# Attention probabilities and v as plain fp32: one product with the values of both heads per key block, in a two-layer trunk on one core

## The chip, the cores and the metric

One core of a Trainium2 chip runs the whole program. The metric is the device time of one execution in microseconds (us); the kernel before was run three times. The engines are named as in the profile: PE (TensorE, products and transposes), PEld (PE's weight loads), DVE (VectorE), ACT (ScalarE), POOL (GpSimd) and SP (SyncE, which issues the DMAs).

## The reference

A trunk of two residual layers over 1024 tokens of width 1024. Layer 0 mixes tokens by a chunked gated MLP, layer 1 by attention; both are followed by an MLP of width 4096. The change touches attention alone: 16 heads of 64, three dilation patterns g, each with its own q, k and v. A block of 128 queries sees its own block of keys and, where there is one, the block before it.

```python
B_PATTERNS = ((128, 1), (512, 4), (2048, 16))
...
    s = jnp.einsum('bnqrhe,bnkrhe->bnrhqk', qb, kb, preferred_element_type=jnp.float32) * (E ** -0.5)
    s = s + bias
    s = jnp.where(valid[None, :, None, None], s, NEG)
    m = jnp.max(s, axis=-1, keepdims=True)
    p = jnp.exp(s - m)
    l = jnp.sum(p, axis=-1, keepdims=True)
    o = jnp.einsum('bnrhqk,bnkrhe->bnqrhe', p / l, vb.astype(jnp.float32))
...
    wts = jax.nn.softmax(jnp.stack(lses, axis=0), axis=0)[..., None]
    o = jnp.sum(wts * jnp.stack(outs, axis=0), axis=0)
```

The products that the change touches are those of the probabilities p with vb, without the division by l, which the kernel does later when it merges the three patterns.

## The kernel before, in words

Everything is fp32 in memory. A tile of type fp32r holds a rounded fp32 number that PE takes as one operand. To keep the precision, a number x is split into hi, x as fp32r, and lo, what is left, as fp32r again: `split` (lines 102 and 103) writes hi by a cast on ACT and lo by a subtraction on DVE. The large products take three of the four combinations of hi and lo (line 1134 for the projections).

Attention works in 24 rounds, `order`: 8 pairs of heads (hp), and in each the patterns 2, 1, 0. Two streams of work are woven together by a list of slots, 8 for a round. The first is `project()`: it makes q, k and v of the later rounds, one step being the three products of 512 columns for one block k (psq, psk, psv). The second, `attend`, puts its functions into a slot at one of three positions. When a slot is run, the functions of positions 0 and 1 are called, then three steps of `project()`, then those of position 2, then three steps more. The framework may shift an instruction by a few places from that.

For a round, `values()` (at the round's start, position 2) transposes vT of both heads, 128 columns of both together, into two PSUM banks (psvt, kind "tr", of which there are two) and splits them into v. Before, v has 256 columns for a block of keys, in the order hi of head 0, lo of head 0, lo of head 1, hi of head 1, so that 128 neighbouring columns hold hi and lo of one head. Then for each of the two heads e:

- `scores(m)` (position 0) makes the scores of query blocks 2m and 2m+1 (sc, lines 1207 and 1208), DVE adds the bias and takes the extreme (line 1214), ACT takes Exp (p, line 1216).
- `transposes(m)` (position 2) transposes a pack of 3 or 4 blocks of p into a "tr" bank (pT, lines 1239 and 1242) and splits it into pThi and pTlo. A pack has 512 columns, or 384; patterns 0 and 1 have four packs for a head, pattern 2 has two.
- `weighted(m)` (position 1, one slot later) multiplies the pack with v into the head's two PSUM banks pv (line 1262). The stationary operand is hi and lo of v, 128 columns, the moving one 128 or 256 columns of pThi, then of pTlo. So 64 rows of pv hold the product with hi of v, the other 64 that with lo of v. After the last pack, ACT copies one half of the rows to oT (line 1279), and DVE adds the other half (line 1280), for each of the two banks.

After the three patterns `merge` scales the oT tiles and adds them up.

Of the kernel before, what the change touches and what calls it, by code (L numbers as in the profile page):

```python
# [35 lines left out]
def trunk(ctx: ExitStack, tc: tile.TileContext, x, c, ada_w, ada_b, ln_g, ln_b, a_w_in, a_b_in,  # L36
# [1010 lines left out]
    def attention(before):  # L1047
# [6 lines left out]
        with ExitStack() as ph:  # L1054
# [113 lines left out]
            def attend(n, oT_of):  # L1168
# [5 lines left out]

                @at(base, 2)
                def values():
                    my["v"] = vs = qp.tile([P, NT, 4, HEAD], F32R, name=f"v_{hp}_{g}", tag="v")
                    for b in range(2):
                        pst = bank("tr", f"psvt_{hp}_{g}_{b}")
                        for t in range(4):  # L1180
                            t0 = (4 * b + t) * P
                            T.transpose(pst[:, t * P : (t + 1) * P], my["vT"][:, t0 : t0 + P], ident[:])
                        split(vs[:, 4 * b : 4 * b + 4, 0:4:3, :], vs[:, 4 * b : 4 * b + 4, 1:3, :],
                              pst[:].rearrange("p (t e c) -> p t e c", e=2, c=HEAD))

                for e in range(2):
                    h = 2 * hp + e
                    rows = slice(e * HEAD, (e + 1) * HEAD)
                    probs, pvs, st = {}, [], dict(begun=[False, False])

                    def scores(m, e=e, h=h, rows=rows, probs=probs, st=st):
                        if m == 0:
                            if e == 0:
                                my["stat"] = qp.tile([P, 2, 2, NT], F32, name=f"stat_{hp}_{g}", tag="stat", bufs=3)
                            st["bias"] = qp.tile([P, width], F32, name=f"bias_{h}_{g}", tag="bias")
                            G.tensor_scalar(st["bias"][:], (far if g == 2 else near)[:],
                                            -8.0 * DILATION[g] * 2.0 ** (-8.0 * (h + 1) / N_HEADS), 1.0, ALU.mult, ALU.mult)
                        scb, used = bank("sc", f"sc_{h}_{g}_{m}"), 0
                        stat = my["stat"]
                        spans = []  # L1200
                        for t in (2 * m, 2 * m + 1):
                            w = 2 * P if has[t] else P
                            sl = slice(used, used + w)
                            used += w
                            k0 = (t - 1) * P if has[t] else t * P
                            tq, keys = slice(t * P, (t + 1) * P), my[f"k{e}"]
                            T.matmul(scb[:, sl], my[f"q{e}"][:, tq], keys[:, k0 : k0 + w], start=True, stop=False)
                            T.matmul(scb[:, sl], my["qlo"][e][:, tq], keys[:, k0 : k0 + w], start=False, stop=True)  # L1208
                            spans.append((t, w, sl))
                        for t, w, sl in spans:  # L1210
                            pr = qp.tile([P, 2 * P], F32, name=f"p_{h}_{g}_{t}", tag="p", bufs=4)
                            col = (t % 2) * 4 + t // 2 if g == 1 else t
                            nm, l = stat[:, 0, e, col : col + 1], stat[:, 1, e, col : col + 1]
                            V.tensor_tensor_reduce(out=pr[:, 0:w], in0=scb[:, sl], in1=st["bias"][:, width - w :], scale=-0.125, scalar=3e38,  # L1214
                                                   op0=ALU.add, op1=ALU.min, accum_out=nm)
                            A.activation(pr[:, 0:w], pr[:, 0:w], AF.Exp, bias=nm, scale=-1.0, accum_out=l)  # L1216
                            probs[t] = pr


                    if g == 0:  # L1220
                        packs = [[(2 * m, True, 0), (2 * m + 1, m < 3, 2 * P)] for m in range(4)]
                        when = [1, 2, 3, 3]
                    elif g == 1:
                        packs = [[(2 * m, True, 0), (2 * m + 1, False, 2 * P)] for m in range(4)]
                        when = [0, 1, 2, 3]
                    else:
                        packs = [[(4 * m + t, False, t * P) for t in range(4)] for m in range(2)]
                        when = [1, 3]
                    total = [0, 0]
                    for t, nxt, _ in sum(packs, []):  # L1230
                        for b in {t // 4, (t + nxt) // 4}:
                            total[b] += 2
                    st["left"] = total
                    pT = {}

                    def transposes(m, h=h, probs=probs, packs=packs, pT=pT):
                        pst = bank("tr", f"pT_{h}_{g}_{m}")
                        for t, nxt, o in packs[m]:
                            T.transpose(pst[:, o : o + P], probs[t][:, P : 2 * P] if has[t] else probs[t][:, 0:P], ident[:])
                            end = o + P  # L1240
                            if nxt:
                                T.transpose(pst[:, o + P : o + 2 * P], probs[t + 1][:, 0:P], ident[:])
                                end = o + 2 * P
                        hi = work.tile([P, HALF], F32R, name=f"pThi_{h}_{g}_{m}", tag="h")
                        lo = qp.tile([P, HALF], F32R, name=f"pTlo_{h}_{g}_{m}", tag="pTlo")
                        split(hi[:, 0:end], lo[:, 0:end], pst[:, 0:end])
                        pT[m] = (hi, lo)

                    def weighted(m, e=e, h=h, rows=rows, packs=packs, pT=pT, pvs=pvs, st=st):
                        if m == 0:  # L1250
                            pvs.extend(bank("pv", f"pv_{h}_{g}_{b}") for b in range(2))
                        begun, left = st["begun"], st["left"]
                        for t, nxt, o in packs[m]:
                            stt = my["v"][:, t, 2 * e : 2 * e + 2, :].rearrange("p a c -> p (a c)")
                            for x_ in pT[m]:
                                pieces = [(t * P, o, P * (1 + nxt))]
                                if nxt and t % 4 == 3:
                                    pieces = [(t * P, o, P), ((t + 1) * P, o + P, P)]
                                for q0, o_, w_ in pieces:
                                    b = q0 // HALF  # L1260
                                    left[b] -= 1
                                    T.matmul(pvs[b][:, q0 % HALF : q0 % HALF + w_], stt, x_[:, o_ : o_ + w_],  # L1262
                                             start=not begun[b], stop=left[b] == 0, skip_group_check=True)
                                    begun[b] = True
                        if m < len(packs) - 1:
                            return
                        oT = oT_of(e)
                        main, rest = (slice(0, 64), slice(64, P)) if e == 0 else (slice(64, P), slice(0, 64))
                        for b in range(2):
                            if g == 0:  # L1270
                                dst = oT[rows, b * HALF : (b + 1) * HALF]
                                sa, sb = pvs[b][rest, :], pvs[b][main, :]
                            elif g == 1:
                                dst = by_pos(oT[rows, :], g)[:, 2 * b : 2 * b + 2, :]
                                sa, sb = (pvs[b][r, :].rearrange("p (r i) -> p r i", r=2) for r in (rest, main))
                            else:
                                dst = by_pos(oT[rows, :], g)[:, 4 * b : 4 * b + 4, :, :]
                                sa, sb = (pvs[b][r, :].rearrange("p (a b i) -> p a b i", a=4, b=2) for r in (rest, main))
                            A.copy(dst, sa)
                            V.tensor_tensor(dst, dst, sb, op=ALU.add)  # L1280

                    for m in range(4):
                        at(base + 4 * e + m, 0)(lambda m=m, f=scores: f(m))
                    for m, w in enumerate(when):
                        at(base + 4 * e + w, 2)(lambda m=m, f=transposes: f(m))
                        at(base + 4 * e + w + 1, 1)(lambda m=m, f=weighted: f(m))
# [179 lines left out]
```

## Time and profile before

| what | value |
|---|---|
| time, median of 3 runs | 2845.51 us (2842.47 to 2847.93) |
| span of the profiled execution | 2841.6 us; its own device time is not given apart from the three runs |
| granted clock of PE, mean | 0.992 |
| PE busy | 2752.7 us, 97% of the span, 13290 products |
| DVE busy | 1944.5 us, 68% |
| ACT busy | 1413.9 us, 50% |
| POOL busy | 220.1 us, 8% |
| DMA | 384.15 MB, 135 GB/s on average |

The span goes from the first to the last instruction of the profiled execution. Engines work side by side, so busy times don't add up to the span. Products on PE overlap one another in their records: what one costs is seen in the distance between starts, not in its duration. In a list of groups a row has the line, engine, operation, out<-in names, shape and count, then the busy time and the mean duration in ns, then the idle time of the engine before them and what ended it. In a timeline a row has the start, the duration and the instruction. Names are those of the program without the buffer number.

### The profile page before, as it was taken

The numbers are of one execution on the slowest core, as the hardware profiler recorded it, in microseconds if no ns is written. First come the engines' busy times: TensorE is split into PE (matmuls) and PEld (weight loads), VectorE is DVE, ScalarE is ACT, GpSimd is POOL, SyncE is SP. The second block draws the span as 40 slices with busy tenths as digits, with TensorE's granted clock in tenths as the row PEclk, the third lists the DMA queues.
The fourth block names the chain that finished last, engine by engine and source line by source line (L and its number), as shares of the span: only waits on it lengthen the run. The fifth ranks groups of instructions, "written<-read, shape, count | busy, mean of one in ns | idle before, by whom it ended". The sixth has DMA issues, their size and how long they took to land.

```text
span 2841.6 us, 36856 instructions
## 1 busy us (share of the span) xinstructions
PE 2752.7 (97%) x13290; PEld 2277.9 (80%) x13290; DVE 1944.5 (68%) x3485; ACT 1413.9 (50%) x2613; POOL 220.1 (8%) x163
## 2 busy tenths in 40 slices
PE   6999999999999999999999999999999999999997
PEld 5777878887888878888888888888877788878886
DVE  6786798777877674656555555555659976577776
ACT  3334375555434455555555555555564755544431
POOL 1021000000000043101000000010201000000000
PEclk9999999999999999999999999999999999999999
DMA  7533346668846343212121212121315564485561
GB/s 253 171 109 106 119 152 223 216 219 277 286 153 201 126 148 105 61 39 68 38 61 39 69 31 69 38 69 31 91 39 178 170 208 158 151 303 189 171 214 60
DMA packets 300186, 384.15 MB, mean 135 GB/s; under 512 B 47532, under 2 KB 172884, under 8 KB 300004
## 3 DMA queue, kind: packets, MB, share of 16 engines
q1 hardware_dynamic: 300004, 381.80, 42.0%
q8 instruction: 104, 1.70, 0.2%
q14 instruction: 78, 0.64, 0.1%
HBM read 297.77 MB, written 83.97 MB: 134 GB/s over the span
## 4 chain that ended last, share of the span: by engine, by line
PE 73%; DVE 11%; DMA 7%; ACT 5%; issue 2%; POOL 2%; SPq 0%; DVEq 0%; ACTq 0%; POOLq 0%
PE psd L938 21%; PE psua L782 10%; PE psv L1134 8%; PE psq L1134 7%; PE psk L1134 5%; PE psuc L782 5%; DMA adaw<-in_ada_w_dram 3%; PE psd_wout L356 3%; PE psub L782 2%; PE pv L1262 2%; PE psd_wo L356 2%; ACT p L1216 1%; DVE adaacc L128 1%; PE psu L356 1%; PE sc L1208 1%
## 5 line engine op out<-in xcount | busy, mean ns | idle before, releaser
L782 PE MATMUL psua<-right,left 128*128 128x512 f32 x1536 | 364.0, 391 | 3.4 <-ACT right L102 1.8
L938 PE MATMUL psd<-rhi,lhi 128*128 128x512 f32 x896 | 351.0, 392 | 2.1 <-ACT part L813 2.1
L938 PE MATMUL psd<-rlo,lhi 128*128 128x512 f32 x896 | 350.9, 392 | 1.2 <-DVE rlo L103 1.1
L938 PE MATMUL psd<-rhi,llo 128*128 128x512 f32 x896 | 350.5, 391 | 0.0
L782 PEld LDWEIGHTS psua<-right,left 128*128 128x128 f32 x1536 | 287.3, 188 | 65.5 <-DVE right L103 3.1
L1216 ACT ACTIVATE p<-p,stat 128x128 f32<-128x128 f32 (+1 forms) x384 | 170.4, 445 | 237.6 <-DVE stat L1214 235.7
L1134 PE MATMUL psv<-hT,wv_hi 128*128 128x512 f32 x768 | 246.0, 401 | 3.2 <-DVE qlo L103 3.2
L1134 PE MATMUL psq<-hT,wq_hi 128*128 128x512 f32 x768 | 246.3, 402 | 0.0
L1134 PE MATMUL psk<-hT,wk_hi 128*128 128x512 f32 x768 | 246.0, 401 | 0.0
L103 DVE TENSOR_TENSOR pTlo<-pT,pThi 128x512 fp32r<-128x512 f32 (+1 forms) x160 | 98.2, 621 | 179.1 <-ACT pThi L102 178.5
L938 PEld LDWEIGHTS psd<-rhi,lhi 128*128 128x128 f32 x896 | 169.3, 189 | 38.4 <-ACT part L813 2.9
L938 PEld LDWEIGHTS psd<-rlo,lhi 128*128 128x128 f32 x896 | 169.1, 189 | 37.0 <-DVE rlo L103 2.2
L938 PEld LDWEIGHTS psd<-rhi,llo 128*128 128x128 f32 x896 | 169.2, 189 | 35.3
L782 PE MATMUL psuc<-right,left 128*128 128x512 f32 x768 | 188.9, 392 | 0.0
L128 DVE SCALAR_TENSOR_TENSOR adaacc<-adaw,silu_c,adaacc 128x512 f32<-128x512 f32 x168 | 133.4, 805 | 64.1 <-DMA adaw<-in_ada_w_dram 63.4
L782 PEld LDWEIGHTS psuc<-right,left 128*128 128x128 f32 x768 | 144.4, 189 | 30.4 <-DVE right L103 0.5
L1214 DVE CUSTOM_DVE_ANT_0 p<-sc,bias 128x128 f32<-128x128 f32 (+1 forms) x384 | 119.7, 347 | 68.6 <-PE sc L1208 66.2
L1134 PEld LDWEIGHTS psv<-hT,wv_hi 128*128 128x128 f32 x768 | 135.6, 189 | 26.1 <-issue 2.8
L1134 PEld LDWEIGHTS psk<-hT,wk_hi 128*128 128x128 f32 x768 | 136.5, 189 | 22.6
L1134 PEld LDWEIGHTS psq<-hT,wq_hi 128*128 128x128 f32 x768 | 135.7, 189 | 22.2
L1134 PE MATMUL psq<-hT,wq_lo 128*128 128x512 f32 x384 | 151.4, 394 | 0.0
L1134 PE MATMUL psv<-hT,wv_lo 128*128 128x512 f32 x384 | 150.6, 392 | 0.0
(250 smaller groups left out, 5843.1 us busy)
## 6 DMA issues: line engine op xcount, KB each, us to landing
lraw<-forms SPq DMA_DIRECT2D x112, 512.0 KB, 3.7
adaw<-in_ada_w_dram SPq DMA_DIRECT2D x192, 256.0 KB, 3.2
up<-in_mlp_w_up_dram SPq DMA_DIRECT2D x64, 512.0 KB, 3.8
forms<-s SPq DMA_DIRECT2D x128, 256.0 KB, 2.4
rraw<-in_mlp_w_down_dram SPq DMA_DIRECT2D x64, 512.0 KB, 4.5
forms<-part SPq DMA_DIRECT2D x96, 256.0 KB, 2.5
spill<-acc SPq DMA_DIRECT2D x24, 512.0 KB, 2.7
wq_raw<-in_b_w_qkv_dram SPq DMA_DIRECT2D x24, 512.0 KB, 3.7
```

Of the source, the lines that this page charges most:

```text
L103: return first, lo_engine.tensor_tensor(lo, src, hi, op=ALU.subtract)
L128: ins = V.scalar_tensor_tensor(acc[:], raw[:], silu_c[:, k : k + 1], acc[:], ALU.mult, ALU.add)
L356: T.matmul(dst, s[a], m[b], start=(n == 0), stop=(n == last))
L782: T.matmul(acc, w[:, a, k, :], right[p][:, b, k, :], start=p in (1, 2, 5) and k + a + b == 0, stop=k == 3 and a == 1, skip_group_check=True)
L938: T.matmul(sums[kind, m][:], l[a][:, k, m * P : (m + 1) * P], r[b][:, k, :], start=p in (1, 5, 2, 3) and kp + k + a + b == 0, stop=kp == K ...
L1134: T.matmul(p[:], wu[a][:, k * P : (k + 1) * P], hT[half][b][:, k, :], start=k + c_ == 0, stop=k == KD - 1 and c_ == 2)
L1208: T.matmul(scb[:, sl], my["qlo"][e][:, tq], keys[:, k0 : k0 + w], start=False, stop=True)
L1214: V.tensor_tensor_reduce(out=pr[:, 0:w], in0=scb[:, sl], in1=st["bias"][:, width - w :], scale=-0.125, scalar=3e38, op0=ALU.add, op1=ALU.m ...
L1216: A.activation(pr[:, 0:w], pr[:, 0:w], AF.Exp, bias=nm, scale=-1.0, accum_out=l)
L1262: T.matmul(pvs[b][:, q0 % HALF : q0 % HALF + w_], stt, x_[:, o_ : o_ + w_], start=not begun[b], stop=left[b] == 0, skip_group_check=True)
```

## The change

- v is one fp32 tile with 128 columns for a block of keys, the 64 of head 0 and the 64 of head 1; one copy on ACT for a bank takes the place of cast and subtraction.
- The transposed probabilities are one fp32 tile, pTs. One copy takes the place of cast and subtraction, on ACT for an odd pack and on DVE for an even one.
- A pack has one product with v for each piece where it had two. The stationary operand is v of both heads, the moving one the probabilities of the head e; only the 64 rows of pv that belong to e are used.
- Those rows are copied from PSUM to oT in one step, by ACT for bank 0 and by DVE for bank 1.

```diff
                 def values():
-                    my["v"] = vs = qp.tile([P, NT, 4, HEAD], F32R, name=f"v_{hp}_{g}", tag="v")
+                    my["v"] = vs = qp.tile([P, NT, P], F32, name=f"v_{hp}_{g}", tag="v")
...
-                        split(vs[:, 4 * b : 4 * b + 4, 0:4:3, :], vs[:, 4 * b : 4 * b + 4, 1:3, :],
-                              pst[:].rearrange("p (t e c) -> p t e c", e=2, c=HEAD))
+                        A.copy(vs[:, 4 * b : 4 * b + 4, :].rearrange("p t c -> p (t c)"), pst[:])
...
-                            total[b] += 2
+                            total[b] += 1
...
-                        hi = work.tile([P, HALF], F32R, name=f"pThi_{h}_{g}_{m}", tag="h")
-                        lo = qp.tile([P, HALF], F32R, name=f"pTlo_{h}_{g}_{m}", tag="pTlo")
-                        split(hi[:, 0:end], lo[:, 0:end], pst[:, 0:end])
-                        pT[m] = (hi, lo)
+                        pT[m] = work.tile([P, HALF], F32, name=f"pTs_{h}_{g}_{m}", tag="h")
+                        (A.copy if m % 2 else V.tensor_copy)(pT[m][:, 0:end], pst[:, 0:end])
...
-                            stt = my["v"][:, t, 2 * e : 2 * e + 2, :].rearrange("p a c -> p (a c)")
-                            for x_ in pT[m]:
...
+                            stt = my["v"][:, t, :]
...
+                                T.matmul(pvs[b][:, q0 % HALF : q0 % HALF + w_], stt, pT[m][:, o_ : o_ + w_],
+                                         start=not begun[b], stop=left[b] == 0, skip_group_check=True)
...
-                            A.copy(dst, sa)
-                            V.tensor_tensor(dst, dst, sb, op=ALU.add)
+                            (V.tensor_copy if b else A.copy)(dst, src)
```

The rows below stand in the order of one engine's program, with the line, the instruction and the size of what it writes; numbers at the end of a name tell tiles apart. The first place is on PE, where the first pack of head 0 in pattern 1 is weighted. Before:

```order
L1207 MATMUL sc_1_1_9245<-k_0_1_8858,q_0_1_8628 128x256
L1208 MATMUL sc_1_1_9245<-k_0_1_8858,qlo_1_8453 128x256
L1262 MATMUL pv_1_0_9256<-pThi_1_0_9232,v_1_9213 128x256
L1262 MATMUL pv_1_0_9256<-pTlo_1_0_9233,v_1_9213 128x256
L1262 MATMUL pv_1_0_9256<-pThi_1_0_9232,v_1_9213 128x128
L1262 MATMUL pv_1_0_9256<-pTlo_1_0_9233,v_1_9213 128x128
L1134 MATMUL psq_0_0_9203<-hT_0_0_8565,wq_0_hi 128x512
```

Four products of the pack stand between the scores and the projection. On PE now:

```order
L1206 MATMUL sc_1_1_9211<-k_0_1_8856,q_0_1_8628 128x256
L1207 MATMUL sc_1_1_9211<-k_0_1_8856,qlo_1_8453 128x256
L1258 MATMUL pv_1_0_9222<-pTs_1_0_9200,v_1_9183 128x256
L1258 MATMUL pv_1_0_9222<-pTs_1_0_9200,v_1_9183 128x128
L1134 MATMUL psq_0_0_9173<-hT_0_0_8565,wq_0_hi 128x512
```

Two products of the program are left, at the same place. The second place is on DVE, around v and the first pack of the same round (ISA on L1214, later L1213, is the score reduction). Before:

```order
L103 TENSOR_TENSOR qlo_0_8454<-psq_0_1_9121,q_0_0_9120 64x512
L1280 TENSOR_TENSOR oT_2_8998<-oT_2_8998,pv_2_1_9086 64x4x2x64
L103 TENSOR_TENSOR v_1_9213<-psvt_1_0_9214,v_1_9213 128x4x128
L103 TENSOR_TENSOR v_1_9213<-psvt_1_1_9221,v_1_9213 128x4x128
L103 TENSOR_TENSOR pTlo_1_0_9233<-pT_1_0_9228,pThi_1_0_9232 128x384
L1214 ISA p_1_2_9250,stat_1_9172<-sc_1_1_9245,bias_1_9173 128x128
```

The two subtractions for v and the one for the pack stand ahead of the next score reduction. On DVE now:

```order
L1274 COPY oT_2_8984<-pv_2_1_9068 64x4x2x64
L103 TENSOR_TENSOR qlo_0_8454<-psq_0_1_9099,q_0_0_9098 64x512
L1244 COPY pTs_1_0_9200<-pT_1_0_9196 128x384
L1213 ISA p_1_2_9216,stat_1_9148<-sc_1_1_9211,bias_1_9149 128x128
L1213 ISA stat_1_9148 128x1
```

The subtractions for v are gone, the copy of the pack stands where its subtraction stood, and the copy to oT takes the place of the addition. On ACT at the same place, before:

```order
L1216 ACTIVATE p_1_1_9183,stat_1_9172<-p_1_1_9183,stat_1_9172 128x256
L1279 COPY oT_2_8998<-pv_2_1_9086 64x4x2x64
L102 CAST v_1_9213<-psvt_1_0_9214 128x4x2x64
L102 CAST v_1_9213<-psvt_1_1_9221 128x4x2x64
L102 CAST pThi_1_0_9232<-pT_1_0_9228 128x384
L1216 ACTIVATE p_1_2_9250,stat_1_9172<-p_1_2_9250,stat_1_9172 128x128
```

Between the two Exp (ACTIVATE) stand four copies or casts. On ACT now:

```order
L1215 ACTIVATE p_1_1_9159,stat_1_9148<-p_1_1_9159,stat_1_9148 128x256
L1183 COPY v_1_9183<-psvt_1_0_9184 128x512
L1183 COPY v_1_9183<-psvt_1_1_9190 128x512
L1215 ACTIVATE p_1_2_9216,stat_1_9148<-p_1_2_9216,stat_1_9148 128x128
L1215 ACTIVATE p_1_3_9219,stat_1_9148<-p_1_3_9219,stat_1_9148 128x256
```

Only the two copies of v are left between them; the copy of bank 1 to oT and that of the even pack are on DVE.

More of the change, by code (lines that the diff above doesn't have):

```diff
@@ L1253, in weighted @@
                         for t, nxt, o in packs[m]:
-                            stt = my["v"][:, t, 2 * e : 2 * e + 2, :].rearrange("p a c -> p (a c)")
-                            for x_ in pT[m]:
[L1256 to L1264, printed above, removed]
+                            stt = my["v"][:, t, :]
+                            pieces = [(t * P, o, P * (1 + nxt))]
+                            if nxt and t % 4 == 3:
+                                pieces = [(t * P, o, P), ((t + 1) * P, o + P, P)]
+                            for q0, o_, w_ in pieces:
+                                b = q0 // HALF
+                                left[b] -= 1
+                                T.matmul(pvs[b][:, q0 % HALF : q0 % HALF + w_], stt, pT[m][:, o_ : o_ + w_],
+                                         start=not begun[b], stop=left[b] == 0, skip_group_check=True)
+                                begun[b] = True
                         if m < len(packs) - 1:
@@ L1267, in weighted @@
                         oT = oT_of(e)
-                        main, rest = (slice(0, 64), slice(64, P)) if e == 0 else (slice(64, P), slice(0, 64))
                         for b in range(2):
@@ L1271, in weighted @@
                                 dst = oT[rows, b * HALF : (b + 1) * HALF]
-                                sa, sb = pvs[b][rest, :], pvs[b][main, :]
+                                src = pvs[b][rows, :]
                             elif g == 1:
                                 dst = by_pos(oT[rows, :], g)[:, 2 * b : 2 * b + 2, :]
-                                sa, sb = (pvs[b][r, :].rearrange("p (r i) -> p r i", r=2) for r in (rest, main))
+                                src = pvs[b][rows, :].rearrange("p (r i) -> p r i", r=2)
                             else:
                                 dst = by_pos(oT[rows, :], g)[:, 4 * b : 4 * b + 4, :, :]
-                                sa, sb = (pvs[b][r, :].rearrange("p (a b i) -> p a b i", a=4, b=2) for r in (rest, main))
-                            A.copy(dst, sa)
-                            V.tensor_tensor(dst, dst, sb, op=ALU.add)
+                                src = pvs[b][rows, :].rearrange("p (a b i) -> p a b i", a=4, b=2)
+                            (V.tensor_copy if b else A.copy)(dst, src)
                     for m in range(4):
```

## The prediction

> **What bounds the kernel now.** I read the page's totals first, then the busy slices and the chain of work that ended last.
>
> ```profile
> PE 2752.7 (97%) x13290; PEld 2277.9 (80%) x13290; DVE 1944.5 (68%) x3485; ACT 1413.9 (50%) x2613; POOL 220.1 (8%) x163
> PE   6999999999999999999999999999999999999997
> PEclk9999999999999999999999999999999999999999
> PE 73%; DVE 11%; DMA 7%; ACT 5%; issue 2%; POOL 2%; SPq 0%; DVEq 0%; ACTq 0%; POOLq 0%
> ```
>
> PE is full from end to end at full clock, so a change counts by what it does to PE. The edited code runs only in attention, which lies between 1040 and 2150 us of the span; the view of busy time by stretch gives that stage (busy us and instruction count of PE, PEld, DVE, ACT, POOL, then clock and DMA):
>
> ```profile
> 1040.00:2150.00 1110.00, 1094.09 (x5857) 916.79 (x5858) 626.43 (x1495) 599.61 (x1418) 152.00 (x121) 1.00 0.22 61
> ```
>
> PE is busy 98.6% of it, DVE 56%, ACT 54%. DVE and ACT time is worth nothing here by itself; what they can cost is a wait of PE. The list of waits of the weight loads in that stretch holds those (us in total, times, longest):
>
> ```profile
> PEld pT L1242 <- ACT p L1216: 9.6, 22, 0.7
> PEld pv L1262 <- DVE pTlo L103: 9.2, 19, 0.7
> PEld pT L1239 <- ACT p L1216: 8.4, 22, 0.8
> PEld pT L1239 <- DVE v L103: 7.0, 8, 1.0
> ...
> PEld pv L1262 <- ACT pThi L102: 0.8, 3, 0.4
> PEld pstat L1294 <- DVE pTlo L103: 0.5, 1, 0.5
> ```
>
> Together 35.5 us: all that a shorter way through ACT and DVE could give back. The timeline shows that such a wait delays PE by its length, and what a 128-column product costs in a row:
>
> ```profile
> 1056.82 0.27 PE L1262 MATMUL pv<-pThi,v 128*128 128x128 f32 x1
> 1057.60 0.33 PE L1262 MATMUL pv<-pTlo,v 128*128 128x128 f32 x1 [0.51 <-DVE pTlo L103]
> 1057.77 0.28 PE L1262 MATMUL pv<-pThi,v 128*128 128x128 f32 x1
> ...
> 1058.33 0.28 PE L1262 MATMUL pv<-pTlo,v 128*128 128x128 f32 x1
> ```
>
> The second product starts 0.78 us after the first. The last two rows shown are 0.56 us apart with five steps between them: 0.112 us each. Durations overlap, so I price PE by distances between starts.
>
> **What a product costs.** The same timeline where a pack of pattern 1 is weighted, then eight transposes of v elsewhere:
>
> ```profile
> 1136.33 0.28 PE L1208 MATMUL sc<-k,qlo 128*128 128x256 f32 x1
> 1136.44 0.28 PE L1262 MATMUL pv<-pThi,v 128*128 128x256 f32 x1
> 1136.56 0.28 PE L1262 MATMUL pv<-pTlo,v 128*128 128x256 f32 x1
> 1136.68 0.22 PE L1262 MATMUL pv<-pThi,v 128*128 128x128 f32 x1
> 1136.74 0.27 PE L1262 MATMUL pv<-pTlo,v 128*128 128x128 f32 x1
> 1136.85 0.68 PE L1134 MATMUL psq<-hT,wq_hi 128*128 128x512 f32 x2
> 1137.36 0.39 PE L1134 MATMUL psq<-hT,wq_lo 128*128 128x512 f32 x1
> 1137.59 0.40 PE L1134 MATMUL psq<-hT,wq_hi 128*128 128x512 f32 x1
> ...
> 1409.91 1.03 PE L1182 MATMUL psvt<-ident,vT 128*128 128x128 f32 x8
> ```
>
> 512 columns take 0.23 us (1137.36 to 1137.59) and 256 take 0.117 (three steps, 1136.33 to 1136.68): the stream, about 0.45 ns a column. 128 columns take 0.06 once and 0.11 otherwise: there the load of 128 weights, one per 0.11 us, sets the pace. Behind a narrow product three psq products take 0.74 us (1136.85 to 1137.59) instead of 3 x 0.23, so 0.05 more.
>
> **The change on PE.** Per pack, hi and lo products with v become one fp32 product. Counts and forms of the hi half (the lo half has the same):
>
> ```profile
> L1262 PE MATMUL pv<-pThi,v 128*128 128x128 f32 x240 | 53.5, 252 | 0.0
> L1262 PE MATMUL pv<-pThi,v 128*128 128x256 f32 x160 | 44.3, 287 | 0.2 <-ACT pThi L102 0.2
> ```
>
> So 800 products go and 400 come, 160 of 256 columns and 240 of 128. But the compiled program of the changed kernel holds 13,290 products and 13,290 weight loads, exactly as many as the page counts before: each fp32 product is carried out as two loads and two products. Halving the products in the source saves no instruction on PE. What is open is how long each of these 800 is; no row of before has a plain fp32 product. Lower end: as now, one stream of its columns, total change 0. Upper end: two streams each. The reason for it is in the kernel: an fp32r operand carries only part of an fp32 number, which is why hi and lo are kept, and a full product of two such numbers is four partial ones; two instructions cover the halves of v, so each must pass the probabilities' halves, two streams. The nearest rows, the only ones where PE takes unsplit fp32, are the transposes: eight in 1.03 us, the last lasting 0.27, make (1.03 - 0.27) / 7 = 0.109 us for 128 columns, twice the 0.06 of an fp32r product; this leans the same way, though the weight load would explain it too. I take two streams.
>
> The price then: a 256-column product takes two streams of 512, 2 x 0.23 = 0.46, against 2 x 0.117 now: +0.226, times 160 = +36 us. A 128-column product takes two streams of 256, 2 x 0.117 = 0.234, against 2 x 0.112 (in a row), or 0.06 + 0.11 + 0.05 = 0.22 (one pair): +0.01, times 240 = +2 us. PE term +38, between 0 and +38 by these rows.
>
> The Trainium skill, page "FP8 and Floating Point Precision", section "TensorE Precision Notes", says that a true fp32 product goes through the array four times, high and low part of one operand with high and low part of the other. No run here shows it yet; by that rule the sum is that of my upper end, without it that of the lower.
>
> **ACT and DVE.** What they do for this now, and the nearest row for an fp32 copy out of PSUM on DVE:
>
> ```profile
> L102 ACT CAST pThi<-pT 128x512 fp32r<-128x512 f32 x80 | 46.9, 586 | 48.4 <-PE pT L1242 35.2 <-PE pT L1239 12.9
> L102 ACT CAST pThi<-pT 128x384 fp32r<-128x384 f32 x80 | 38.4, 480 | 39.0 <-PE pT L1239 38.7
> L102 ACT CAST v<-psvt 128x512 fp32r<-128x512 f32 x48 | 25.8, 591 | 3.9 <-PE psvt L1182 3.5
> L1279 ACT COPY oT<-pv 64x512 f32<-64x512 f32 x96 | 86.4, 900 | 8.8 <-DVE oT L1350 5.6 <-PE pv L1262 1.6
> L103 DVE TENSOR_TENSOR pTlo<-pT,pThi 128x512 fp32r<-128x512 f32 x80 | 55.1, 689 | 111.2 <-ACT pThi L102 110.9
> L103 DVE TENSOR_TENSOR pTlo<-pT,pThi 128x384 fp32r<-128x384 f32 x80 | 44.3, 554 | 67.9 <-ACT pThi L102 67.6
> L103 DVE TENSOR_TENSOR v<-psvt,v 128x512 fp32r<-128x512 f32 x48 | 30.9, 687 | 2.4 <-ACT v L102 1.7
> L1280 DVE TENSOR_TENSOR oT<-oT,pv 64x512 f32<-64x512 f32 x96 | 90.1, 938 | 76.8 <-ACT oT L1279 75.8
> L462 DVE COPY vz<-psvt x16: 674/685/692, 62.7 to 149.5; 128x512 f32<-128x512 f32 x16
> ```
>
> Odd packs go to ACT (32 of 512, 48 of 384 columns: 32 x 0.586 + 48 x 0.480 = 42 us), even ones to DVE (48 x 0.685 + 32 x 0.554 = 51), v to ACT (48 x 0.591 = 28), and the 96 row copies are shared (48 x 0.900 = 43 and 48 x 0.938 = 45). ACT falls from 197 to 113 us, DVE from 220 to 96. All of it lies beside PE: 0 by itself. Bounds for a copy are the removed instructions of its own size, which stood in the same queues, so no engine gets fuller.
>
> What it does give is shorter chains to PE. pT to pv went through a cast and then a subtraction (0.586 + 0.689), now through one copy: at least 0.55 us earlier, against waits of at most 0.7. Of 10.5 us (the three waits on pTlo and pThi) I take 8. The eight waits of pT for v lose the subtraction, 8 x 0.69 = 5.5 of 7.0. The 44 waits on Exp (18.0 us, 0.41 each) shrink because the weighted product that stands between scores and transposes lasts 0.23 longer in patterns 0 and 1, and ACT has less queued ahead: 0.2 each, 8.5. Sum -22, between 0 and -35.5. A copy on DVE waits for PE's transposes where the subtraction waited for ACT's cast; behind it stand the next score reductions, which thus come earlier, not later. The order of the DMAs is the same but for one store of a spilled tile two places later, and nothing waits on SP: 0.
>
> **Sum.** +38 - 22 = +16 on a span of 2841.6, so 2857.6. The profiled execution's own time isn't given; the median run, 2845.5, is 3.9 above its span, and I keep that: 2861.
>
> **The rivals.**
> - One stream per instruction (faster). PE term 0, the 22 us come back: 2823.5. For it: instruction counts are equal, and the transposes' 0.109 can be all weight load. Against it: lo x lo and the cross terms must be computed somewhere. It decides if a 256-column product shows starts 0.12 apart. 0.10.
> - All waits go (no change). +38 - 35.5: 2848. For it: shorter chains everywhere. Against it: Exp and the score reductions are untouched. 0.12.
> - Nothing comes back: the waits move from pTlo to Exp or the next copy. 2883.5. 0.12.
> - The weights of fp32 halves aren't loaded under the stream before them: 800 x 0.11 = 88 us more, 2950. Against it: every load now, those of the fp32 transposes too, is overlapped. 0.04.
>
> **The numbers.** My forecast has 0.62. The measurement tells about 0.2% from no change, 5.7 us: 2839.8 to 2851.2 is "same". Faster 0.10 (one stream), same 0.12 (all waits go), slower 0.78 (the rest). The range goes from just under the case of all waits gone, 2845, to just over nothing back, 2887; one stream and uncovered loads stay outside.
>
> **What would show it.** Two records for each pv product, starts 0.23 apart for 256 columns and 0.12 for 128; again 13,290 products; the attention stretch some 16 us longer, all else unmoved; waits of pv on its copy under 3 us and of pT on v under 2. It is wrong if pv starts stay 0.12 apart at 256 columns, or if waits on Exp grow instead of halving.

## The result and the profile after

The changed kernel took 2856.27 us, the median of 5 runs (2850.88 to 2859.89), against 2845.51 for the kernel before (5 runs, 2840.70 to 2847.93). The ratio is 1.0043, 95% interval 1.0027 to 1.0059: slower by 0.4%, some 11 us. The forecast was 2861. The profiled execution took 2856.27 us with a span of 2854.2, so 2.1 us lie around the span.

The page's first line, then attention in the view of busy time by stretch (columns as before):

```profile
PE 2778.2 (97%) x13290; PEld 2303.3 (81%) x13290; DVE 1825.5 (64%) x3309; ACT 1332.7 (47%) x2485; POOL 216.4 (8%) x163
...
1040.00:2160.00 1120.00, 1114.44 (x5858) 939.01 (x5857) 505.95 (x1320) 517.47 (x1288) 147.32 (x121) 1.00 0.22 61
```

DVE lost 119 us and ACT 81, and the kernel got slower: PE's number of products and loads is unchanged, and PE is now busy 99.5% of that stretch where it was 98.6% of its own before. The forms of the products with v, and the timeline where a pack of pattern 1 is weighted and where one of pattern 2 is:

```profile
L1258 PE MATMUL pv<-pTs,v 128*128 128x256 f32 x320 | 88.1, 381 | 0.1
...
L1258 PE MATMUL pv<-pTs,v 128*128 128x128 f32 x480 | 75.5, 277 | 0.0
```

```profile
1055.32 1.10 PE L1258 MATMUL pv<-pTs,v 128*128 128x128 f32 x8
1056.18 0.71 PE L1134 MATMUL psk<-hT,wk_hi 128*128 128x512 f32 x2
1056.72 0.39 PE L1134 MATMUL psk<-hT,wk_lo 128*128 128x512 f32 x1
...
1099.44 0.82 PE L1258 MATMUL pv<-pTs,v 128*128 128x256 f32 x4
1100.01 0.71 PE L1134 MATMUL psk<-hT,wk_hi 128*128 128x512 f32 x2
1100.56 0.40 PE L1134 MATMUL psk<-hT,wk_lo 128*128 128x512 f32 x1
1100.79 0.40 PE L1134 MATMUL psk<-hT,wk_hi 128*128 128x512 f32 x1
```

The 160 products of 256 columns are 320 records, the 240 of 128 are 480: two for each. A pack of pattern 1 (one product of 256 and one of 128, named together in the row of 4) with the three products of the projection behind it takes from 1099.44 to 1100.79, 1.35 us. Before, it took from 1136.44 to 1137.59, 1.15: 0.20 more, for one product of 256 columns. In pattern 2 a pack of four products with the two products of the projection behind it takes from 1055.32 to 1056.72, 1.40 us; eight fp32r products by 0.112 and the 0.51 of the same two products (1136.85 to 1137.36 before) make 1.41: nothing more. These packs are no exception. Over all packs that stand ahead of the projection and meet no wait, from the first product with v to the fourth product behind, the median went from 1.15 to 1.36 us with one product of each width, and stayed at 1.64 with four products of 128.

The waits of the weight loads in attention (the window ends 15 us later than that of the list before, since attention ends later):

```profile
PEld pT L1241 <- ACT p L1215: 6.1, 17, 0.5
...
PEld pT L1238 <- ACT v L1183: 2.5, 8, 0.3
PEld pT L1238 <- ACT p L1215: 1.7, 5, 0.9
...
PEld pstat L1288 <- DVE pTs L1244: 0.6, 1, 0.6
PEld pv L1258 <- ACT pTs L1244: 0.6, 2, 0.4
PEld pv L1258 <- DVE pTs L1244: 0.2, 1, 0.2
```

They add up to 11.7 us where they were 35.5. So 160 x 0.20 = 32 us more work on PE and 23.8 us less waiting make +8. Attention itself, from the first transpose of v to the start of the last product with v, went from 1073.4 us (1048.0 to 2121.4) to 1082.1 (1046.9 to 2129.0): +8.7. The rest of the output product behind it is 3.7 us longer: its weight loads wait 2.2 us more (11.7 instead of 9.5), and the granted clock was 0.91 between 2160 and 2200 us where it was 0.96. That makes 12.4 of the 12.6 us by which the span is longer; the median is longer by 10.8.

The rounds show it by pattern. These are the starts of the transposes of v, in the timeline of the kernel before for a round of pattern 2, one of 1, one of 0 and the next:

```profile
1455.60 1.04 PE L1182 MATMUL psvt<-ident,vT 128*128 128x128 f32 x8
...
1499.66 1.03 PE L1182 MATMUL psvt<-ident,vT 128*128 128x128 f32 x8
...
1545.15 1.03 PE L1182 MATMUL psvt<-ident,vT 128*128 128x128 f32 x8
...
1590.84 1.03 PE L1182 MATMUL psvt<-ident,vT 128*128 128x128 f32 x8
```

And in that of the changed kernel:

```profile
1457.93 1.04 PE L1182 MATMUL psvt<-ident,vT 128*128 128x128 f32 x8
...
1500.83 1.03 PE L1182 MATMUL psvt<-ident,vT 128*128 128x128 f32 x8
...
1547.11 1.04 PE L1182 MATMUL psvt<-ident,vT 128*128 128x128 f32 x8
...
1594.85 1.04 PE L1182 MATMUL psvt<-ident,vT 128*128 128x128 f32 x8
```

Pattern 2, which has products of 128 columns only, went from 44.06 to 42.90 us; pattern 1, with eight products of 256 in a round, from 45.49 to 46.28; pattern 0, with twelve, from 45.69 to 47.74. Together that is +1.68 for this head pair. Times 8 it would be 13, more than the 8.7 that attention gained in all: the first and the last pair differ from those between, and in the last round, where no projection is left, pattern 0 got 1 us shorter (36.7 to 35.7). One change was a gain in one pattern and a loss in the other two.

### The profile page after: what moved, and what is told of

Same layout as the page of the kernel before. It is cut to its first block, busy times and chain, and to the rows that moved or that the text cites. A ratio compares the mean times of both kernels' runs of the same rounds, so it can differ in the third digit from the quotient of the medians.

```text
span 2854.2 us, 36472 instructions
## 1 busy us (share of the span) xinstructions
PE 2778.2 (97%) x13290; PEld 2303.3 (81%) x13290; DVE 1825.5 (64%) x3309; ACT 1332.7 (47%) x2485; POOL 216.4 (8%) x163
## 4 chain that ended last, share of the span: by engine, by line
PE 81%; DVE 10%; DMA 5%; ACT 3%; issue 1%; SPq 0%; DVEq 0%; POOL 0%; ACTq 0%; POOLq 0%
PE psd L938 21%; PE psua L782 10%; PE psq L1134 9%; PE psv L1134 9%; PE psk L1134 7%; PE psuc L782 5%; PE pv L1258 4%; DMA adaw<-in_ada_w_dram 3%; PE psd_wout L356 3%; PE psub L782 2%; PE psd_wo L356 2%; PE sc L1207 1%; PE pT L1238 1%; PE sc L1206 1%; PE psu L356 1%; DVE adaacc L128 1%
## 5 line engine op out<-in xcount | busy, mean ns | idle before, releaser
L1213 DVE CUSTOM_DVE_ANT_0 p<-sc,bias 128x128 f32<-128x128 f32 (+1 forms) x384 | 120.0, 348 | 180.8 <-PE sc L1207 178.1
L1134 PEld LDWEIGHTS psk<-hT,wk_hi 128*128 128x128 f32 x768 | 137.1, 189 | 23.8
L1134 PE MATMUL psk<-hT,wk_lo 128*128 128x512 f32 x384 | 150.7, 392 | 0.0
```

Source lines behind the costliest of these rows:

```text
L1134: T.matmul(p[:], wu[a][:, k * P : (k + 1) * P], hT[half][b][:, k, :], start=k + c_ == 0, stop=k == KD - 1 and c_ == 2)
```

## The experiments

The theory: fp32 products of 256 columns cost PE 0.2 us each, and the shorter ways from PSUM through ACT and DVE give 22 us back. The first four kernels ran on one chip beside the kernel before (median 2843.08 us), the next four on another (2842.32). The times below are of the whole program, most of which the change does not touch. Where these other stages blur the comparison, attention is given by itself, measured as above, from one profiled execution of each kernel; the granted clock was 1.00 there in all of them, and the rounds between the first and the last head pair repeat within some tenths of a us.

**Long ways with fp32 products.** All three ways out of PSUM get their second step back:

```diff
-                        A.copy(vs[:, 4 * b : 4 * b + 4, :].rearrange("p t c -> p (t c)"), pst[:])
+                        src = pst[:].rearrange("p (t c) -> p t c", c=P)
+                        A.copy(vs[:, 4 * b : 4 * b + 4, 0, :], src)
+                        V.tensor_tensor(vs[:, 4 * b : 4 * b + 4, 1, :], src, vs[:, 4 * b : 4 * b + 4, 0, :], op=ALU.max)
...
-                        (A.copy if m % 2 else V.tensor_copy)(pT[m][:, 0:end], pst[:, 0:end])
...
+                        A.copy(first[:, 0:end], pst[:, 0:end])
+                        V.tensor_tensor(pT[m][:, 0:end], pst[:, 0:end], first[:, 0:end], op=ALU.max)
...
-                            (V.tensor_copy if b else A.copy)(dst, src)
+                            A.copy(dst, src)
+                            V.tensor_tensor(dst, dst, src, op=ALU.max)
```

> The changed kernel with the fp32 products kept and each of the three ways out of PSUM made as long as before: v, the transposed probabilities and the output rows each go through a copy on ACT and then a pass on DVE that reads PSUM and the copy (the larger of the two, which is the same number). Theory (fp32 products cost PE about 32 us more, and the shorter ways through ACT and DVE give about 22 back): the cost alone is seen, 2845.5 + 32 = 2877, at least 2870, since the longer products may still cover some waits on Exp. Rival 1 (the products cost only some 11 us and the ways out of PSUM give nothing): 2856, as the changed kernel. Rival 2 (all of the gain comes from the longer products covering waits, not from the shorter ways): 2856 to 2860.

Measured: 2860.24 us, ratio to before 1.0063 (1.0049 to 1.0076). By the time this is the second rival, and the interval overlaps that of the changed kernel. Attention says otherwise: 1092.7 us, 10.6 more than with the short ways and 19.3 more than before. Outside attention this profiled execution was 6.5 us shorter than that of the changed kernel, at a mean granted clock of 0.993 against 0.991. So the short ways are worth some 10 us with fp32 products too. The waits in its attention stretch:

```profile
PEld pT L1240 <- DVE v L1185: 7.1, 8, 1.0
PEld pT L1243 <- ACT p L1217: 6.7, 18, 0.7
PEld pT L1240 <- ACT p L1217: 6.6, 17, 1.1
PEld pv L1262 <- DVE pTs L1248: 5.5, 12, 0.6
...
PEld pstat L1293 <- DVE pTs L1248: 0.4, 1, 0.4
```

26.3 us instead of 35.5: with nothing shortened, the longer products alone took 9.2 us of waits away, 4.7 of them on Exp (18.0 to 13.3) and 4.6 on the packs. The wait on v stayed. So 32 us of work less 9.2 of waits would be +22.8, where +19.3 came.

**Short ways with pairs of fp32r products.**

```diff
-                    my["v"] = vs = qp.tile([P, NT, P], F32, name=f"v_{hp}_{g}", tag="v")
+                    my["v"] = vs = qp.tile([P, NT, P], F32R, name=f"v_{hp}_{g}", tag="v")
...
-                            total[b] += 1
+                            total[b] += 2
...
-                        pT[m] = work.tile([P, HALF], F32, name=f"pTs_{h}_{g}_{m}", tag="h")
+                        pT[m] = work.tile([P, HALF], F32R, name=f"pTs_{h}_{g}_{m}", tag="h")
...
-                            for q0, o_, w_ in pieces:
+                            for q0, o_, w_ in pieces * 2:
```

> The changed kernel with v and the probabilities as fp32r, written by one cast each, and each product made twice with the same operands, so PE gets 800 fp32r products as before; the lo parts are left out of the computation. Theory: PE costs what it did before and the shorter ways give their part back: 2845.5 - 22 = 2823, in 2818 to 2830; the waits of the weight loads in attention fall from 35.5 us to about 12. Rival 1 (shorter ways give nothing): 2845. Rival 2 (the gain comes from longer products covering waits): 2838 to 2845. The distance to the changed kernel is the price of the fp32 products, 32 us by the theory.

Measured: 2833.58 us, ratio 0.9968 (0.9955 to 0.9981), so -9 and not -22. Attention is 12.6 us shorter than before. Its waits:

```profile
PEld pT L1241 <- ACT p L1215: 10.3, 20, 0.7
PEld pT L1238 <- ACT p L1215: 8.8, 16, 1.6
...
PEld pT L1238 <- ACT v L1183: 2.6, 8, 0.3
...
PEld pv L1258 <- DVE pTs L1244: 0.8, 2, 0.5
PEld pstat L1288 <- DVE pTs L1244: 0.7, 1, 0.7
...
PEld pv L1258 <- ACT pTs L1244: 0.2, 1, 0.2
```

The waits on packs and on v are all but gone (17.5 to 4.3 us), those on Exp are as long as before (18.0 to 19.1). So freeing ACT does nothing for Exp by itself. The waits add up to 23.4 us, 12.1 less than before, which is what attention gained. Against this kernel the change's fp32 products cost 1.0043 - 0.9968 = 0.75%, 21 us, and attention alone has 1082.1 - 1060.8 = 21.3: 32 us of PE less the 11.7 us of waits that they cover (23.4 to 11.7).

**One fp32r product.** As above, without the `* 2`.

> The changed kernel with v and the probabilities as fp32r, written by one cast each, and one fp32r product where it has an fp32 one; the lo parts are left out of the computation. This is what the change would be worth if one fp32 product cost one product. Theory (PE sets the time; 160 products of 256 columns at 0.117 us instead of 0.43, 240 of 128 at 0.11 or less instead of 0.22): 2856 - 50 - 26 = 2780, up to 2800 if waits that the longer products covered come back. Rival (ACT and DVE chains, not PE, have become the bound of attention): no lower than 2820.

Measured: 2785.54 us, ratio 0.9799 (0.9784 to 0.9814), in the theory's range: PE sets the time, not the ways through ACT and DVE. Its page shows the 400 products fewer that the change did not bring:

```profile
PE 2703.0 (97%) x12890; PEld 2235.3 (80%) x12890; DVE 1822.2 (65%) x3309; ACT 1329.5 (48%) x2485; POOL 218.5 (8%) x163
```

**fp32 in pattern 2 alone.** The kernel before, with the change's branches where g is 2:

```diff
...
-                            total[b] += 2
+                            total[b] += 1 if g == 2 else 2
...
+                        if g == 2:
+                            one = work.tile([P, HALF], F32, name=f"pTs_{h}_{g}_{m}", tag="h")
+                            (A.copy if m % 2 else V.tensor_copy)(one[:, 0:end], pst[:, 0:end])
+                            pT[m] = (one,)
+                            return
...
+                            if g == 2:
+                                (V.tensor_copy if b else A.copy)(dst, pvs[b][rows, :].rearrange("p (a b i) -> p a b i", a=4, b=2))
+                                continue
```

> The kernel before with the change made in pattern 2 alone, where all products with v have 128 columns; patterns 0 and 1 keep hi and lo. Theory (an fp32 product of 128 columns costs PE no more than the two fp32r ones, both paced by a weight load every 0.11 us; of 256 columns 0.2 us more): pattern 2's rounds shorten by 1.2 us as they did in the changed kernel (44.1 to 42.9 us from one round's first transpose of v to the next), the others stay: 2845.5 - 8 x 1.2 = 2836, faster than both kernels. Rival (the rounds of pattern 2 gained because the work of their neighbours on ACT and DVE fell): 2841 to 2846.

Measured: 2826.40 us, ratio 0.9946 (0.9930 to 0.9962): faster than both kernels, and by more than expected. The rounds in its timeline:

```profile
1449.08 1.04 PE L1182 MATMUL psvt<-ident,vT 128*128 128x128 f32 x8
...
1491.98 1.03 PE L1182 MATMUL psvt<-ident,vT 128*128 128x128 f32 x8
...
1536.86 1.04 PE L1182 MATMUL psvt<-ident,vT 128*128 128x128 f32 x8
...
1582.55 1.04 PE L1182 MATMUL psvt<-ident,vT 128*128 128x128 f32 x8
```

Pattern 2's round is 42.90 us as forecast, pattern 0's 45.69 as before, but pattern 1's fell too, from 45.49 to 44.88. A round's last output rows are copied at the start of the next, so pattern 2's shorter copy helps pattern 1; the kernel below that shortens this copy alone bears this out, with 44.87 us for the same round of pattern 1. Eight times 1.16 + 0.61 is 14 us; the ratio says 15, and attention is 14.9 shorter.

**Which way gives the gain?** Three kernels shorten one way each in the kernel before. First the transposed probabilities:

```diff
-                        lo = qp.tile([P, HALF], F32R, name=f"pTlo_{h}_{g}_{m}", tag="pTlo")
-                        split(hi[:, 0:end], lo[:, 0:end], pst[:, 0:end])
-                        pT[m] = (hi, lo)
+                        (A.copy if m % 2 else V.tensor_copy)(hi[:, 0:end], pst[:, 0:end])
+                        pT[m] = (hi, hi)
```

> The kernel before with the transposed probabilities written by one cast (odd packs on ACT, even ones on DVE) and the cast tile used for both products; lo of the probabilities is left out of the computation. Theory (each way out of PSUM gives back its own wait): the 10.5 us of waits of pv fall to about 1.5, so 2843 - 9 = 2834; the waits on v (7.0) and on Exp (18.0) stay. Rival (the waits only move on): the waits on Exp grow by what pv loses, and the time stays at 2843.

Measured: 2841.07 us, ratio 0.9994 (0.9985 to 1.0003): no difference that can be told. In attention it is 3.7 us. Its waits of packs:

```profile
PEld pv L1261 <- DVE pThi L1245: 7.1, 16, 0.8
...
PEld pstat L1293 <- DVE pThi L1245: 0.6, 1, 0.6
PEld pv L1261 <- ACT pThi L1245: 0.6, 2, 0.4
```

8.3 us are left of 10.5, nearly all behind the one copy on DVE. Then v, by one cast (`A.copy` into a tile of 128 columns per block instead of `split`):

> The kernel before with v written by one cast on ACT; its 128 columns for a key block are those of both heads, and lo of v is left out of the computation (the added half of pv is the other head's). Theory: the wait of pT on v falls from 7.0 us to 2.5, as in the changed kernel, and the time by as much, 2839. Rival (the wait is the addition to oT, which stands ahead of the subtractions on DVE, not the subtractions): the 7.0 us stay, and so does the time.

Measured: 2839.78 us, ratio 0.9991 (0.9982 to 0.9999), so 2.5 us, a gain that is barely clear of noise. Attention is 6.4 us shorter, as much as its waits fell (35.5 to 29.0); the rest of this profiled execution ran at a lower granted clock, 0.989 in the mean. In its waits v's 7.0 us became 3.7, and the packs' 9.2 on DVE became 5.4 although nothing was done to them:

```profile
PEld pv L1261 <- DVE pTlo L103: 5.4, 13, 0.7
PEld pT L1238 <- ACT v L1183: 3.7, 8, 0.6
```

And the output rows:

```diff
-                            A.copy(dst, sa)
-                            V.tensor_tensor(dst, dst, sb, op=ALU.add)
+                            (V.tensor_copy if b else A.copy)(dst, sb)
```

> The kernel before with the head's rows copied to oT in one step, bank 0 by ACT and bank 1 by DVE, and the addition dropped; the product with lo of v is left out of the computation. Theory: nothing on PE waits for oT itself, so only what stands behind it gains: the wait on v falls by about half, 3.5 us, and the waits on Exp by 2, 2838. Rival (this is the largest of the three, since it takes 1 us off each of two engines ahead of v and Exp): all of v's 7.0 and half of Exp's 18 go, 2827.

Measured: 2834.24 us, ratio 0.9972 (0.9960 to 0.9984): the largest of the three, and between theory and rival, with a bit more for v and nothing for Exp:

```profile
PEld pT L1242 <- ACT p L1216: 10.1, 20, 0.7
PEld pv L1262 <- DVE pTlo L103: 8.0, 18, 0.7
PEld pT L1239 <- ACT p L1216: 7.2, 19, 0.7
...
PEld pT L1239 <- DVE v L103: 1.9, 8, 0.2
```

Attention is 8.5 us shorter. The addition to oT took 1 us on DVE and stood ahead of v's subtractions, as the order of the program shows, and it had to wait for ACT's copy of the same rows. DVE in the kernel before, where a round of pattern 1 begins (its transposes of v start at 1499.66):

```profile
1500.43 1.07 DVE L1280 TENSOR_TENSOR oT<-oT,pv 64x512 f32<-64x512 f32 x1 [1.37 <-ACT oT L1279]
1501.53 1.29 DVE L103 TENSOR_TENSOR v<-psvt,v 128x512 fp32r<-128x512 f32 x2
```

The same place with the rows copied in one step:

```profile
1495.27 1.04 DVE L1279 COPY oT<-pv 64x512 f32<-64x512 f32 x1
...
1495.95 1.03 PE L1182 MATMUL psvt<-ident,vT 128*128 128x128 f32 x8
...
1497.21 1.29 DVE L103 TENSOR_TENSOR v<-psvt,v 128x512 fp32r<-128x512 f32 x2 [0.90 <-ACT v L102]
```

The copy waits for nothing on ACT and is done before v's cast begins. The subtractions start 1.26 us after the first transpose instead of 1.87, which is 0.61 earlier in each of eight such rounds, and the waits on v fall by 5.1 us (7.0 to 1.9), although v is still split.

**What paces an fp32 product of 128 columns.** The kernel with pattern 2 alone changed, and each of its products cut in two:

```diff
+                                if g == 2:
+                                    pieces = [(t * P, o, HEAD), (t * P + HEAD, o + HEAD, HEAD)]
```

> The kernel with the change in pattern 2 alone, and there each fp32 product of 128 columns cut into two of 64. Theory (a weight load every 0.11 us sets the pace of an fp32 product of 128 columns, and two streams of 128 take nearly as long): the starts of pv's records stay 0.11 us apart with 64 columns, twice as many of them, and 128 products x 0.22 us = 28 us come on top: 2826 + 28 = 2854. Rival (the streams alone set the pace): records 0.055 us apart, no more time, 2826.

Measured: 2853.76 us, ratio 1.0039 (1.0026 to 1.0053), 27 us above the uncut kernel (26 in attention), as the theory had it. The timeline where a pack is weighted:

```profile
1056.48 1.96 PE L1272 MATMUL pv<-pTs,v 128*128 128x64 f32 x16
1058.24 0.70 PE L1134 MATMUL psk<-hT,wk_hi 128*128 128x512 f32 x2
```

Sixteen records in 1.76 us, 0.11 each: the same with half the columns, so the columns don't set the pace. What each record has besides is its weight load. That a record could have a least time of its own is no better explanation: in the prediction's rows one product of 128 columns follows another by 0.06 us, behind products of 256 columns that left time for its load. The Trainium skill's page "TensorE: Matmul & The Clock Gate", section "LDWEIGHTS (loading the stationary operand)", gives a load as its columns divided by 1.2, in ns, 107 for 128; the 0.11 agrees.

## Why the prediction was right

The sign, the size and the reason held: +16 was forecast, +10.8 came. Part of the size is luck. In attention, the only stage for which the sum has a term, it was +8.7; the output product gave 3.7 more, for which there was no term, and 1.8 were lost again around the span.

- **Two streams for each of two instructions**: right by the time. Two records a product, 13,290 again, and with 256 columns a record every 0.21 us where an fp32r product takes 0.117. Whether that is two passes or one at half the pace, the runs don't show. The PE term was +32 and not +38: I priced a 256-column product at 2 x 0.23, from 512-column rows, and the timeline gives a pack 0.20 more, not the 0.24 that my rows gave. The rule of four passes in the Trainium skill's page "FP8 and Floating Point Precision", section "TensorE Precision Notes", agrees: by my 0.45 ns a column, 4 x 256 is 0.46 us, and the measured price is 0.117 x 2 + 0.20 = 0.43.
- **Nothing for 128 columns**: right, shown by pattern 2's rounds and by the cut products.
- **ACT and DVE beside PE**: right. Of 81 and 119 us less there (84 and 124 forecast) only the waits of PE that went with them came back: 12 us where the products stayed as they were.
- **Waits give back 22**: the sum was right (23.8), and so were the sizes of its parts: 9.1 us on the packs (8 forecast), 4.5 on v (5.5), 10.2 on Exp (8.5). The reasons for the parts were not, and that the sum came out is luck to that extent. The 8 us that I gave to the one copy of a pack: alone, that copy took 2.2 us of waits, and the one cast of v took more off the packs (9.2 to 5.4 on DVE) than that. What kept v late was DVE's queue, above all the addition to oT, for which I had no term; that step alone gave 8 us. I had put oT at zero because nothing on PE waits for it by name; what is queued behind it does. The 8.5 us on Exp I put down to the longer products of patterns 0 and 1 and to a freer ACT. Counted by round, the waits on Exp fell from 7.1 to 0.9 us in pattern 2, which has no product of 256 columns, and from 9.7 to 6.6 in pattern 1. In pattern 1 the fp32 products do it: with the long ways 6.0 are left, with short ways alone 10.9. In pattern 2 neither does it alone (6.2 and 7.1), only both together, and why stays open. Nor does a shorter product bring the waits back: the single fp32r products leave 12.3 of the 18.0.
- **The signs**: the copy of a pack was to cost pv under 3 us of waits, and it does (0.8); v was to cost pT under 2, and it is 2.5. The records of 256 columns start 0.21 apart and those of 128 start 0.11 apart (0.23 and 0.12 forecast).
- **Around the span**: 2.1 us, not 3.9.

The rivals: "one stream per instruction" is what the kernel with pairs of fp32r products measures, 2833.6 and not 2823.5, because without the longer products only 12 of the 22 us come back. "All waits go" did not come, 11.7 us are left; "nothing comes back" neither, and even with the long ways 9.2 us came back. The weight loads stayed under the streams: a pack of pattern 1 with four records takes 0.20 us more, and four uncovered loads would be 0.44 on top.

## What to carry to other kernels

Price an fp32 product by what it becomes on PE: here two loads and two products, each taking the time of two streams of its columns. Replacing a pair of fp32r products, it is free at 128 columns, where the weight load sets the pace of both, and costs 0.2 us at 256; so take it where the moving operand is narrow and keep the pair where it is wide (ratio to before 0.9946 here, against 1.0043 with fp32 everywhere). And look at what an operation stands ahead of in its queue: the addition that no one on PE waited for was the step whose removal gave most. Last, where a change touches one stage, compare that stage: in the whole time the long ways of the first experiment moved the ratio by 0.0020, which is within noise; in attention they cost 10.6 us.

## What the runs showed of the hardware

An fp32 product has two records in the trace, each with a weight load of its own. With 128 or with 64 columns the records follow one another by 0.11 us (0.86 us for eight, 1.76 for sixteen); with 256 columns by 0.21 (1099.44, 1099.65, 1099.87 in the pack shown), and a pack takes 0.20 us more than with a pair of fp32r products.

Behind the last record of a pack the next fp32r products start early, but the three of them take 0.78 us (1100.01 to 1100.79) where three by 0.23 take 0.69, and where three behind the pair of fp32r products took 0.74. So the price has to be taken across the whole pack and what follows it, not from where the next product starts.
